# Second feed-forward block: the first sixteen inner tiles through the output weights as seven block products instead of eight, four tiles at a time

## The chip, the core and the metric

The kernel runs on one core of a Trainium2 chip. The metric is device time in microseconds (us); lower is better. The engines of the core are named as in the profile: PE (TensorE, matrix products; PEld is its weight load), DVE (VectorE), ACT (ScalarE), POOL (GpSimd), and SP, whose queue issues the loads. Each engine works through its own list of instructions.

## What is computed

One decoder block on 512 tokens of width 1024: a SwiGLU feed-forward, a token-mixing part and a second SwiGLU feed-forward, each with a modulated RMSNorm in front and a gated residual behind. The change concerns the second feed-forward alone:

```python
def swiglu(u, w_in, w_out):
    a, b = jnp.split(u @ w_in, 2, axis=-1)
    return (jax.nn.silu(a) * b) @ w_out
...
u = modulate(rmsnorm(h, g_norm_ffn2[l]), sh3, sc3)
h = h + 0.5 * gt3 * swiglu(u, w_ffn2_in[l], w_ffn2_out[l])
```

Here `w_in` is 1024 x 5632 and `w_out` 2816 x 1024. All data is float32.

## The kernel before

**Layout.** Features lie on the 128 partitions and the 512 tokens along the free dimension. The residual is eight tiles `H[m]` of 128x512, the normed input eight tiles `UH[k]`/`UL[k]`, and the 2816 inner features make 22 inner tiles.

**Split products.** Each float32 operand is a sum of two parts that TensorE reads as `fp32r`: a high part, made by ACT as a copy (`whi<-raw` for weights, `HI<-hf` for inner tiles), and a low part, made by DVE as the operand minus its high part (`wlo<-raw,whi`, `HK<-hf,HI`). A product is three matmuls: high x high, high x low, low x high.

**Weight stream.** Weights come in chunks of mostly 128x1024. SP loads a chunk into one of a few `raw` buffers (three, and two more, printed as `X`, from the first block product on). `split` then makes its two parts in a ring that holds seven chunks: `split_hi` issues the ACT copy and, if the next chunk is itself a difference of loaded chunks, DVE's subtraction for it (`make`, printed `X<-raw,X`); `split_lo` issues the DVE part. `look(4)`, called ahead of each product, runs this to four chunks ahead of the product about to be issued. `look()` runs three ahead.

**Inner tiles by seven products.** Inner tiles 0 to 3 are computed plainly (`ffn_pair`). From tile 4 on, `duo(j)` makes tiles j and j+1 at once: the inputs and weights are cut into 2x2 blocks, and seven block products replace eight. Each product is 24 matmuls on 256 tokens and uses one chunk, of which four are differences. The banks A, B and C of PSUM collect the products in the order A, B, A, C, A, B, A. Between two products on A its sum so far has to be copied out by ACT: after product 0 (`bank<-bank`, A into C), after product 2 (`u<-bank`) and after product 4 (`u<-bank` again). After product 1 the sum on B is copied (`p<-bank`). The next product on that bank, two products on for A, waits for the copy.

**Deferred work.** `later(n, f)` puts f aside until n more calls of `step()`, which comes after each product. The multiplication of a duo's two tiles (`hf<-sl,hf`) comes one step later, the high part and the low part two steps later.

**Output pass.** The inner tiles go through `w_out` in `PARTS` of 4, 4, 4, 4 and 6 tiles. Before the change each of the first four parts is a plain pass: eight output tiles, four inner tiles, three matmuls on 512 tokens, 96 matmuls and four chunks; DVE adds each result to `H[m]` with the gate (`H<-bank,mod,H`). In the program of before, the plain pass of part 0 follows the plain pairs directly; each later part is preceded by one duo of the next tiles (`pairs_before`). The last part ends the program and is not touched.

**Order.** `manual_schedule` keeps the instructions of each engine in the order in which the Python code issues them. Semaphore waits are put in from the tiles that are read and written.

Of the kernel before, what the change touches and what calls it, by code (L numbers as in the profile page):

```python
# [12 lines left out]
OP = mybir.AluOpType  # L13
# [33 lines left out]
def _fmajor(w, cols):  # L47
    k = w.shape[0] // P
    return w[:, cols].reshape(k, P, len(cols)).transpose(1, 0, 2).reshape(P, -1)
# [3 lines left out]
    return [np.arange(s, s + P) for s in starts]  # L53


def lay_ffn(w_in, w_out, first, plain):

    ins, outs = [], []  # L60
    if first:
        cols = np.concatenate([c for j in range(first) for c in _tiles(j * P, DFF + j * P)])
        for k in range(KT):
            ins.append(w_in[k * P:(k + 1) * P][:, cols])
    for j in range(first, plain):
        for c in _tiles(j * P, DFF + j * P):
            ins.append(_fmajor(w_in, c))
    for j in range(plain, FT, 2):
        for i, c in ((0, 0), (0, DFF), (1, DFF), (1, 0)):
            rows = w_in[i * D // 2:(i + 1) * D // 2]  # L70
            ins.append(np.concatenate([_fmajor(rows, x) for x in _tiles(c + j * P, c + j * P + P)], axis=1))
    for k0, k1 in PARTS:
        for m in range(KT):
            outs.append(_fmajor(w_out[k0 * P:k1 * P], np.arange(m * P, (m + 1) * P)))
    n = KT * (len(PARTS) - 1)
    return ins, [np.concatenate(outs[i:i + 2], axis=1) for i in range(0, n, 2)] + outs[n:]

# [59 lines left out]
class Kernel:  # L137
# [6 lines left out]
    def plan(self):  # L144
# [495 lines left out]

    def ffn_post(self, j, s, pb):
        nc = self.nc
        h = self.fw.tile([P, T], F32, name=("hf", "u3")[j % 2])
        nc.vector.tensor_tensor(h, s, pb, op=OP.mult)
        hh, hl = self.HH[j % NH], self.HL[j % NH]
        nc.scalar.activation(hh, h, AF.Copy)
        nc.vector.tensor_tensor(hl, h, hh, op=OP.subtract)

    def ffn_silu(self, j, pa):
        s = self.fw.tile([P, T], F32, name=("sl", "u2")[j % 2])  # L650
        self.nc.scalar.activation(s, pa, AF.Silu)
        return s

# [69 lines left out]
    def duo(self, j, first, last):  # L723
# [13 lines left out]
        c = self.fw.tile([P, 2 * T], F32, name="hf")  # L737
        u2, u3, p5 = (self.fw.tile([P, T], F32, name=x) for x in ("u2", "u3", "p5"))
        q = lambda x: x.rearrange("p (j h t) -> p j h t", j=2, h=2)
        r = lambda x: x.rearrange("p (j t) -> p j t", j=2)  # L740
        silu = lambda h, bank: nc.scalar.activation(q(s)[:, :, h, :], r(bank), AF.Silu)

        def mult():
            v.tensor_tensor(c, s, c, op=OP.mult)

        def high():
            copy(self.HHall[:, j % NH * T:(j % NH + 2) * T], c)

        def low():
            x = slice(j % NH * T, (j % NH + 2) * T)  # L750
            v.tensor_tensor(self.HLall[:, x], c, self.HHall[:, x], op=OP.subtract)


        for i, (bank, u, start) in enumerate(((A, blk(lo4, T1), True), (B, S[0], True), (A, S[1], False),
                                              (C, blk(hi4, T1), False), (A, S[2], False), (B, S[3], False),
                                              (A, blk(hi4, T2), False))):
            if i == 6:
                v.tensor_tensor(q(c)[:, :, 1, :], r(u3), r(p5), op=OP.add)
            self.look(4)
            self.product(bank, u, start)  # L760
            self.step()
            if i == 0:
                copy(C, A)
                if first:
                    first()
                    self.free += self.rawx
            elif i == 1:
                copy(p5, B)
            elif i == 2:
                copy(u2, A)  # L770
            elif i == 3:
                silu(0, C)
            elif i == 4:
                copy(u3, A)
            elif i == 6:
                silu(1, A)
                v.tensor_tensor(q(c)[:, :, 0, :], r(B), r(u2), op=OP.add)
        if last:
            mult()
            high()  # L780
# [1 line left out]
        else:  # L782
            self.later(1, mult)
            self.later(2, high)
            self.later(2, low)

    def ffn2(self):
        self.put, self.now = [], 0
        bk = [self.nb() for _ in range(4)]
        self.head(2, bk, AF.Silu)  # L790
        self.todo, last = self.u_steps(2)
# [33 lines left out]
    def ffn(self, n, j, last=None):  # L825
# [10 lines left out]
        for part, (k0, k1) in enumerate(PARTS):  # L836
            tail = part + 1 == len(PARTS)
            while j < pairs_before(n, part):
                if j < PLAIN[n]:
                    self.ffn_pair(j, beside)  # L840
                    j += 1
                else:
                    self.duo(j, last, tail and j + 2 == FT)
                    last = None
                    j += 2
            if n == 0:
                last = self.beside_out(part) or last
            nk = k1 - k0
            hk = [(self.HH[k % NH], self.HL[k % NH]) for k in range(k0, k1)]
            if not tail:  # L850
                for m in range(0, KT, 2):
                    self.look(4)
# [492 lines left out]
    def build(self):  # L1345
# [39 lines left out]
        with self.open_ffn():  # L1385
            self.ada_pool = ExitStack()
            self.adaw = self.ada_pool.enter_context(tc.tile_pool(name="f1a", bufs=4))
            self.put, self.now = [], 0
            self.startup()
            self.ffn(0, FIRST)  # L1390
            self.sums.close()
# [132 lines left out]
def lay_inputs(x, c, positions, w_ada, b_ada, g_norm_ffn1, w_ffn1_in, w_ffn1_out, g_norm_mix, w_in, w_pool,  # L1524
# [4 lines left out]
    f1i, f1o = lay_ffn(A(w_ffn1_in)[0], A(w_ffn1_out)[0], FIRST, PLAIN[0])  # L1529
    f2i, f2o = lay_ffn(A(w_ffn2_in)[0], A(w_ffn2_out)[0], 0, PLAIN[2])  # L1530
    wp = np.zeros((P, 2 * P), np.float32)
    for g in range(4):
        r = 64 * (g % 2)
# [30 lines left out]
```

## Time and profile before

| | us |
|---|---|
| median of 3 runs (lowest, highest) | 1017.11 (1016.72, 1018.24) |
| span of the profiled execution | 1018.4 |
| second feed-forward: first input matmul to last output matmul | 667.2 to 1007.9 |
| plain inner tiles 2 and 3 | 691.4 to 713.2 |
| plain output pass of part 0 | 713.2 to 734.9 |
| three duos (tiles 4 to 9) | 734.9 to 792.7 |
| output passes of parts 1, 2, 3 start at | 792.7, 853.0, 913.3 |
| last part starts at | 973.6 |

The profiled execution lies 1.3 us above the median of the runs; both are of the same program. A view by windows gives each engine's busy time in a stretch. The timeline gives start and duration of single instructions; the duration of one runs some 0.08 us into the next one of the same DVE or ACT, so two that follow each other directly start a little less than one duration apart. For matmuls the distance of two starts is the time that counts, since they are pipelined.

### The profile page before, as it was taken

Reading aid. Unit: us, or ns where it says so; the run is one execution under the profiler, and the core shown is the slowest. Engines: PE = TensorE matmul, PEld = TensorE weight load, DVE = VectorE, ACT = ScalarE, POOL = GpSimd, SP = SyncE. Lnnn points to the kernel's source line nnn. Section 1 sums busy time; section 2 is a strip of 40 time slices with the busy share of each in tenths; the row PEclk is TensorE's granted clock in tenths of the full one; section 3 lists DMA queues with packets and bytes.
Section 4 is the critical chain, followed back from the end, with each engine's and each line's share of the span. In section 5 each row is a group of like instructions: output and inputs, shape, how many; then the busy total and the mean of one; then the engine's idle time right before and its main releaser. Section 6 shows DMA issues by size and latency. Waiting matters only on the chain.

```text
span 1018.4 us, 15580 instructions
## 1 busy us (share of the span) xinstructions
PE 1007.5 (99%) x6364; PEld 913.3 (90%) x6364; DVE 756.1 (74%) x1112; ACT 437.2 (43%) x668; POOL 26.2 (3%) x30
## 2 busy tenths in 40 slices
PE   8999999999999999999999999999999999999997
PEld 7888898989999999889988888998899899998997
DVE  6979879889786776879447776577787776676764
ACT  5453352625444552233414323364366254352553
POOL 0000000000000000007100000000000000000001
PEclk9999999999999999999999999999999999999998
DMA  8856465455533413122154773312243234241312
GB/s 314 287 196 246 136 211 176 175 168 174 168 111 112 147 46 104 52 83 83 32 198 167 248 271 121 117 53 78 88 168 123 80 105 145 84 144 44 111 34 83
DMA packets 43114, 139.61 MB, mean 137 GB/s; under 512 B 4897, under 2 KB 8225, under 8 KB 43042
## 3 DMA queue, kind: packets, MB, share of 16 engines
q1 hardware_dynamic: 42354, 137.95, 40.8%
q8 instruction: 50, 0.82, 0.3%
q10 hardware_dynamic: 688, 0.66, 0.2%
q14 instruction: 22, 0.18, 0.1%
HBM read 135.82 MB, written 2.77 MB: 136 GB/s over the span
## 4 chain that ended last, share of the span: by engine, by line
PE 94%; DVE 4%; ACT 0%; issue 0%; DMA 0%; DVEq 0%; ACTq 0%
PE bank L337 17%; PE bank L338 17%; PE bank L339 17%; PE bank L719 10%; PE bank L721 10%; PE bank L720 10%; PE bank L1494 1%; PE bank L1496 1%; PE bank L1498 1%; PE bank L1090 1%; PE bank L1269 1%; PE bank L1423 1%; PE bank L1270 1%; PE bank L1271 1%; PE bank L1038 1%; DVE wlo L306 1%
## 5 line engine op out<-in xcount | busy, mean ns | idle before, releaser
L306 DVE TENSOR_TENSOR wlo<-raw,whi 128x1024 fp32r<-128x1024 f32 (+6 forms) x173 | 177.4, 1037 | 67.6 <-ACT whi L294 67.1
L294 ACT ACTIVATE whi<-raw 128x1024 fp32r<-128x1024 f32 (+6 forms) x173 | 152.3, 899 | 40.6 <-DVE raw L240 39.0
L337 PE MATMUL bank<-UH,whi 128*128 128x512 f32 (+1 forms) x432 | 158.3, 366 | 0.0
L338 PE MATMUL bank<-UL,whi 128*128 128x512 f32 (+1 forms) x432 | 154.2, 357 | 0.1
L339 PE MATMUL bank<-UH,wlo 128*128 128x512 f32 (+1 forms) x432 | 154.1, 357 | 0.0
L337 PE MATMUL bank<-HI,whi 128*128 128x512 f32 (+1 forms) x406 | 146.6, 361 | 0.0
L338 PE MATMUL bank<-HK,whi 128*128 128x512 f32 (+1 forms) x406 | 146.3, 360 | 0.0
L339 PE MATMUL bank<-HI,wlo 128*128 128x512 f32 (+1 forms) x406 | 146.2, 360 | 0.0
L721 PE MATMUL bank<-UH,wlo 128*128 128x256 f32 x512 | 141.6, 277 | 0.0
L719 PE MATMUL bank<-UH,whi 128*128 128x256 f32 x512 | 141.6, 277 | 0.0
L720 PE MATMUL bank<-UL,whi 128*128 128x256 f32 x512 | 141.6, 277 | 0.0
L306 DVE TENSOR_TENSOR wlo<-X,whi 128x1024 fp32r<-128x1024 f32 (+4 forms) x96 | 105.3, 1103 | 39.0 <-ACT whi L294 38.7
L719 PE MATMUL bank<-SH,whi 128*128 128x256 f32 x384 | 107.1, 279 | 0.1
L720 PE MATMUL bank<-SL,whi 128*128 128x256 f32 x384 | 107.0, 279 | 0.0
L721 PE MATMUL bank<-SH,wlo 128*128 128x256 f32 x384 | 106.9, 278 | 0.0
L294 ACT ACTIVATE whi<-X 128x1024 fp32r<-128x1024 f32 (+4 forms) x96 | 89.9, 958 | 32.1 <-DVE X L240 28.9
L720 PEld LDWEIGHTS bank<-UL,whi 128*128 128x128 f32 x512 | 96.3, 188 | 0.3
L719 PEld LDWEIGHTS bank<-UH,whi 128*128 128x128 f32 x512 | 96.1, 188 | 0.3
L721 PEld LDWEIGHTS bank<-UH,wlo 128*128 128x128 f32 x512 | 96.1, 188 | 0.0
L339 PEld LDWEIGHTS bank<-UH,wlo 128*128 128x128 f32 x432 | 81.3, 188 | 12.1
L338 PEld LDWEIGHTS bank<-UL,whi 128*128 128x128 f32 x432 | 81.2, 188 | 11.7 <-issue 0.5
L337 PEld LDWEIGHTS bank<-UH,whi 128*128 128x128 f32 x432 | 81.2, 188 | 11.3 <-issue 0.5
(225 smaller groups left out, 1746.4 us busy)
## 6 DMA issues: line engine op xcount, KB each, us to landing
ada<-wada SPq DMA_DIRECT2D x47, 512.0 KB, 5.0
raw<-wmix SPq DMA_DIRECT2D x44, 512.0 KB, 3.6
raw<-wf1i SPq DMA_DIRECT2D x34, 512.0 KB, 4.3
raw<-wf2i SPq DMA_DIRECT2D x30, 512.0 KB, 3.5
X<-wf2i SPq DMA_DIRECT2D x14, 512.0 KB, 3.6
cs<-wada SPq DMA_DIRECT2D x12, 512.0 KB, 3.5
AR<-wada SPq DMA_DIRECT2D x12, 512.0 KB, 4.0
raw<-wf2o SPq DMA_DIRECT2D x12, 512.0 KB, 3.6
```

Of the source, the lines that this page charges most:

```text
L294: self.nc.scalar.activation(self.hi[:, y], r[:, x], AF.Copy)
L306: self.nc.vector.tensor_tensor(self.lo[:, y], r[:, x], self.hi[:, y], op=OP.subtract)
L337: M(ps, hi, uh, start=start, stop=False)
L338: M(ps, hi, ul, start=False, stop=False)
L339: M(ps, lo, uh, start=False, stop=stop)
L719: M(o, hi, uh, start=start and p == 0 and k == 0, stop=False, skip_group_check=True)
L720: M(o, hi, ul, start=False, stop=False, skip_group_check=True)
L721: M(o, lo, uh, start=False, stop=k == 3, skip_group_check=True)
L1038: M(S[:, o + i * P:o + i * P + P], qz[:, (2 * i + h) * P:(2 * i + h + 1) * P], k[:, toks], start=True, stop=True)
L1090: M(o, pt[:, blk * P:blk * P + P], v, start=i == 0, stop=i == len(srcs) - 1)
L1269: M(b, self.UH[k][:, c::4], hi, start=k == 0, stop=False)
L1270: M(b, self.UH[k][:, c::4], lo, start=False, stop=False)
```

## The change

The first four output passes of the second feed-forward become `out_quad(k0, gate)`. The four inner tiles and the 512 x 1024 block of output weights are cut into 2x2 blocks, and seven products of 24 matmuls on 256 tokens replace the 96 matmuls on 512 tokens. A sum now fills two banks, so each copy of a bank becomes two. The four sums of inner blocks that the products need are made by `h_sums(k0)`: each is a DVE addition, an ACT high part and a DVE low part. They are put aside with `later` and so fall between the products of the duo that comes ahead of the pass. For part 0 there is now such a duo too. A duo whose second half of tokens is only needed as a sum leaves out the high and low part of that half. Products of inner tiles are kept in `self.kept`, which reuses three tiles that are free by then (`cond`, `cs`, `AR`). Of each four output weight chunks four differences are made, as for the duos, and the whole stream of part 0 to 3 is chunks for seven products.

```diff
     def plan(self):
...
-                plain(outs[part * KT // 2:(part + 1) * KT // 2] if part + 1 < len(PARTS) else outs[-KT:])
+                put = blocks if n and part + 1 < len(PARTS) else plain
+                put(outs[part * KT // 2:(part + 1) * KT // 2] if part + 1 < len(PARTS) else outs[-KT:])
...
 def pairs_before(n, part):
...
-    return k1 if part + 1 == len(PARTS) or (n == 2 and part == 0) else k1 + 2
+    return k1 if part + 1 == len(PARTS) else k1 + 2
...
     def duo(self, j, first, last):
...
+        ts = slice(0, 1 if self.kept and j % 4 == 0 and j < PARTS[-1][0] else 2)
...
+    def h_sums(self, k0):
...
+        def add(o, x, y, op):
+            v.tensor_tensor(o, x, y, op=op)
+
+        def high(i, s):
+            nc.scalar.activation(to[i][0], s, AF.Copy)
+
+        def low(i, s):
+            v.tensor_tensor(to[i][1], s, to[i][0], op=OP.subtract)
+
+        for n, what in enumerate(((lambda: add(h22, h21, h22, OP.add), lambda: high(0, h22)),
+                                  (lambda: add(h21, h11, h21, OP.subtract), lambda: high(2, h21), lambda: low(0, h22)),
+                                  (lambda: add(h11, h22, h11, OP.subtract), lambda: high(1, h11), lambda: low(2, h21)),
+                                  (lambda: add(h12, h12, h11, OP.subtract), lambda: high(3, h12), lambda: low(1, h11)),
+                                  (lambda: low(3, h12),))):
+            for f in what:
+                self.later(2 + n, f)
+
+    def out_quad(self, k0, gate):
...
+        def product(banks, u, start):
+            w = self.take()
+            for m in range(4):
+                o = banks[m // 2][:, m % 2 * HT:m % 2 * HT + HT]
+                for k in range(2):
+                    (hi, lo), (uh, ul) = w[2 * m + k], u[k]
+                    M(o, hi, uh, start=start and m % 2 == 0 and k == 0, stop=False, skip_group_check=True)
+                    M(o, hi, ul, start=False, stop=False, skip_group_check=True)
+                    M(o, lo, uh, start=False, stop=k == 1, skip_group_check=True)
+
+        def to_h(m, src, t):
+            h = self.H[m][:, t]
+            v.scalar_tensor_tensor(h, src, gate[:, m:m + 1], h, op0=OP.mult, op1=OP.add)
+
+        for i, (bank, u, start) in enumerate(((A, blk(k0, T1), True), (B, G[0], True), (A, G[1], False),
+                                              (C, blk(k0 + 2, T1), False), (A, G[2], False), (B, blk(k0, T2), False),
+                                              (A, blk(k0 + 2, T2), False))):
+            if i == 6:
+                for b in range(2):
+                    v.tensor_tensor(D[b][:, :, 1, :], p5[b], D[b][:, :, 1, :], op=OP.add)
+            self.look(4)
+            product(bank, u, start)
+            self.step()
+            for b in range(2):
+                if i == 0:
+                    copy(C[b], A[b])
+                elif i == 1:
+                    copy(p5[b], r(B[b]))
+                elif i == 2:
+                    copy(D[b][:, :, 0, :], r(A[b]))
+                elif i == 3:
+                    for m in (2 * b, 2 * b + 1):
+                        to_h(m, C[b][:, m % 2 * HT:m % 2 * HT + HT], T1)
+                elif i == 4:
+                    copy(D[b][:, :, 1, :], r(A[b]))
+                elif i == 5:
+                    v.tensor_tensor(D[b][:, :, 0, :], r(B[b]), D[b][:, :, 0, :], op=OP.add)
+        for m in range(4):
+            to_h(m, A[m // 2][:, m % 2 * HT:m % 2 * HT + HT], T2)
+        for m in range(4):
+            d = D[m // 2][:, m % 2, :, :].rearrange("p h t -> p (h t)")
+            self.later(1 + m // 2, lambda m=m, d=d: to_h(4 + m, d, slice(0, T)))
...
     def ffn(self, n, j, last=None):
...
                 else:
+                    if self.kept and not tail and j == k1:
+                        self.h_sums(k0)
                     self.duo(j, last, tail and j + 2 == FT)
...
+            if not tail and n:
+                self.out_quad(k0, gate)
+                continue
```

Left out are the layout of the weights on the host, the reuse of tiles for `kept`, and places in `duo` where views of tiles change without another instruction.

**ACT in the duo of tiles 16 and 17**, from the high part of the duo before it to about product 4. `u` and `p` are copies of banks, `sl` is the SiLU, `whi` the next weight chunks. Before:

```order
L726 ACTIVATE HI<-hf 128x1024
L726 ACTIVATE p_7630<-bank_100 128x512
L294 ACTIVATE whi<-X 128x896
L294 ACTIVATE whi<-X 128x128
L726 ACTIVATE u_7628<-bank_99 128x512
L294 ACTIVATE whi<-X 128x1024
L741 ACTIVATE sl<-bank_101 128x2x256
L294 ACTIVATE whi<-raw_68 128x1024
L726 ACTIVATE u_7629<-bank_99 128x512
```

and after (`ut`, and the last `HI`, are the high parts of the four sums of `h_sums`):

```order
L735 ACTIVATE HI<-cs 128x1024
L820 ACTIVATE ut<-cs 128x512
L735 ACTIVATE p_7961<-bank_97 128x512
L303 ACTIVATE whi<-X 128x1024
L820 ACTIVATE ut<-cond 128x512
L735 ACTIVATE u_7962<-bank_99 128x2x256
L303 ACTIVATE whi<-X 128x1024
L820 ACTIVATE ut<-cond 128x512
L758 ACTIVATE sl<-bank_102 128x2x256
L303 ACTIVATE whi<-X 128x1024
L820 ACTIVATE HI<-cs 128x2x256
L735 ACTIVATE u_7962<-bank_99 128x2x256
```

Ahead of each copy of a bank now stands the high part of a sum.

**DVE in the same duo**, from the multiplication of the duo before it. Before:

```order
L744 TENSOR_TENSOR hf<-sl,hf 128x1024
L240 TENSOR_TENSOR X<-X 128x1024
L306 TENSOR_TENSOR wlo<-raw_67,whi 128x1024
L751 TENSOR_TENSOR HK<-hf,HI 128x1024
L306 TENSOR_TENSOR wlo<-X,whi 128x896
L306 TENSOR_TENSOR wlo<-X,whi 128x128
L306 TENSOR_TENSOR wlo<-X,whi 128x1024
L306 TENSOR_TENSOR wlo<-raw_68,whi 128x1024
```

and after (the rows of L817 are the additions of `h_sums`, those of L823 its low parts):

```order
L761 TENSOR_TENSOR cs<-sl,cs 128x1024
L249 TENSOR_TENSOR X<-raw_66,X 128x1024
L315 TENSOR_TENSOR wlo<-raw_68,whi 128x1024
L769 TENSOR_TENSOR HK<-cs,HI 128x1024
L817 TENSOR_TENSOR cs<-cond,cs 128x2x256
L315 TENSOR_TENSOR wlo<-X,whi 128x1024
L817 TENSOR_TENSOR cond<-cond 128x2x256
L823 TENSOR_TENSOR G_5879<-cs,ut 128x512
L249 TENSOR_TENSOR X<-X 128x1024
L315 TENSOR_TENSOR wlo<-X,whi 128x1024
L817 TENSOR_TENSOR cond<-cs,cond 128x2x256
L823 TENSOR_TENSOR G_5883<-cond,ut 128x512
```

Each addition stands behind the low part of a weight chunk, and that one behind the addition of the step before.

**ACT from plain tile 3 into the duo of tiles 4 and 5**, after the change (before, the plain output pass lies between the second `HI` and the copy of a bank):

```order
L655 ACTIVATE HI<-cs 128x512
L303 ACTIVATE whi<-X 128x1024
L660 ACTIVATE p_5992<-bank_97 128x512
L303 ACTIVATE whi<-X 128x1024
L655 ACTIVATE HI<-cs 128x512
L303 ACTIVATE whi<-raw_68 128x1024
L303 ACTIVATE whi<-raw_66 128x896
L303 ACTIVATE whi<-raw_66 128x128
L735 ACTIVATE bank_101<-bank_99 128x512
```

The copy of product 0 of the duo (last row) now stands behind three weight chunks and the high part of tile 3.

More of the change, by code (lines that the diff above doesn't have):

```diff
@@ L53, in _tiles, with lay_ffn @@
     return [np.arange(s, s + P) for s in starts]
-def lay_ffn(w_in, w_out, first, plain):
+def lay_ffn(w_in, w_out, first, plain, blocks):
     ins, outs = [], []
@@ L71, in lay_ffn @@
             ins.append(np.concatenate([_fmajor(rows, x) for x in _tiles(c + j * P, c + j * P + P)], axis=1))
+    quads = []
     for k0, k1 in PARTS:
+        if blocks and k1 < FT:
+            for i, c in ((0, 0), (0, 4), (1, 4), (1, 0)):
+                rows = w_out[(k0 + 2 * i) * P:(k0 + 2 * i + 2) * P]
+                quads.append(np.concatenate([_fmajor(rows, x) for x in _tiles(*((c + m) * P for m in range(4)))], axis=1))
+            continue
         for m in range(KT):
             outs.append(_fmajor(w_out[k0 * P:k1 * P], np.arange(m * P, (m + 1) * P)))
+    if blocks:
+        return ins, quads + outs
     n = KT * (len(PARTS) - 1)
@@ L649, in ffn_silu @@
     def ffn_silu(self, j, pa):
-        s = self.fw.tile([P, T], F32, name=("sl", "u2")[j % 2])
+        s = self.fw.tile([P, T], F32, name="sl" if j % 2 == 0 else "u2" if not self.kept else "p5")
         self.nc.scalar.activation(s, pa, AF.Silu)
@@ L767, in duo @@
             elif i == 1:
-                copy(p5, B)
+                copy(p5, r(B))
             elif i == 2:
-                copy(u2, A)
+                copy(u2, r(A))
             elif i == 3:
@@ L787, in ffn2 @@
     def ffn2(self):
         self.put, self.now = [], 0
+        self.kept = [self.cond, self.cs, self.AR]
         bk = [self.nb() for _ in range(4)]
         self.head(2, bk, AF.Silu)
+        self.G = [(self.tp.tile([P, T], F32R, name="ut"), self.fw.tile([P, T], F32R, name=f"G{i}")) for i in range(3)]
         self.todo, last = self.u_steps(2)
```

50 lines of the change are left out of this document (39 added, 11 removed).

## The prediction

> **What bounds the kernel now.** The page's busy times and the chain that ended last come first, then who PE waited for.
>
> ```profile
> span 1018.4 us, 15580 instructions
> PE 1007.5 (99%) x6364; PEld 913.3 (90%) x6364; DVE 756.1 (74%) x1112; ACT 437.2 (43%) x668; POOL 26.2 (3%) x30
> ...
> PE 94%; DVE 4%; ACT 0%; issue 0%; DMA 0%; DVEq 0%; ACTq 0%
> ```
>
> ```profile
> PE bank L1416 <- ACT cond L1414: 3.3, 1, 3.3
> PE bank L1067 <- ACT prob L1055: 0.3, 1, 0.3
> ```
>
> PE is the bound everywhere: 94% of the chain, and its only long wait is 3.3 us at the start. So in the changed stretch fewer matmuls are a gain in full and each wait of PE a loss in full. Next the windows over one period of a plain output pass and two duos.
>
> ```profile
> 853.00:874.80 21.80, 21.80 (x99) 18.04 (x98) 15.17 (x16) 6.63 (x7) 0.00 (x0) 1.00 0.18 53
> 874.80:894.00 19.20, 19.20 (x169) 19.20 (x168) 13.92 (x14) 8.77 (x12) 0.00 (x0) 1.00 0.31 111
> 894.00:913.30 19.30, 19.30 (x172) 19.30 (x170) 14.23 (x16) 11.26 (x15) 0.00 (x0) 1.00 0.47 150
> ```
>
> PE is full at a granted clock of 1.00. DVE (third pair) has 43.3 of the 60.3 us, ACT 26.7.
>
> **What PE saves.** The starts of matmuls (first and last of the stretches) give their prices.
>
> ```profile
> 852.98 0.40 PE L337 MATMUL bank<-HI,whi 128*128 128x512 f32 x1
> ...
> 874.77 0.28 PE L719 MATMUL bank<-UH,whi 128*128 128x256 f32 x1
> ...
> 877.59 0.28 PE L719 MATMUL bank<-SH,whi 128*128 128x256 f32 x1
> ...
> 896.82 0.28 PE L719 MATMUL bank<-SH,whi 128*128 128x256 f32 x1
> ...
> 899.68 0.29 PE L719 MATMUL bank<-SH,whi 128*128 128x256 f32 x1
> ...
> 902.41 0.28 PE L719 MATMUL bank<-UH,whi 128*128 128x256 f32 x1
> ...
> 913.29 0.40 PE L337 MATMUL bank<-HI,whi 128*128 128x512 f32 x1
> ```
>
> A plain pass is 21.79 us for 96 matmuls, 227 ns each. Products 3 to 6 of the duo take 10.88 us for 96 on 256 tokens, 113 ns each; product 1, the dearest, 2.86 us for 24, 119 ns each. The 168 matmuls of a quad cost 19.0 us at the one and 20.0 at the other. I take 19.05: the quad's chunks go through `blocks`, which places them in the ring as for the duos, and six of a duo's seven products run at or near 113. Saved: 4 x 2.74 = 11.0 us, and 0.3 more, since a duo's first product lasts 2.82 us behind a plain pass (874.77 to 877.59) and 2.72 behind products. At the dear price it would be 7.2.
>
> **What DVE and ACT get.** Prices: 1024 elements start 1.14 us apart on DVE (rows below), and these groups give the smaller ones.
>
> ```profile
> L758 DVE TENSOR_TENSOR hf<-u,p 128x512 f32<-128x512 f32 x9 | 6.2, 686 | 0.0
> L863 DVE SCALAR_TENSOR_TENSOR H<-bank,mod,H 128x512 f32<-128x512 f32 x25 | 18.5, 749 | 20.0 <-PE bank L339 20.0
> L489 DVE SCALAR_TENSOR_TENSOR H<-bank,mod,H 128x256 f32<-128x256 f32 x10 | 4.8, 482 | 4.5 <-PE bank L339 4.5
> ```
>
> Less the 0.08 us by which neighbours overlap that is 0.60, 0.67 and 0.40. Per quad DVE gets three more low parts and four `make` (7 x 1.14 = 8.0), eight instructions for the sums less half a low part (4.3), four additions of sums of products (2.4), and eight updates of H of 256 and four of 512 instead of eight of 512 (0.5): 15.2 us. 43.3 + 15.2 = 58.5 us per period, against 57.4 of PE (two duos of 19.2 and a quad). So DVE is full, and for four periods that alone would leave 4 x (60.3 - 58.5) = 7.2 of the 11.3 us. ACT rises by three weight chunks (2.9), four high parts (2.0) and eight copies (4.0) to some 36 us: no bound as a sum. SP's list holds the same loads, with part 0's output chunks behind those of tiles 4 and 5; the windows' DMA share of 0.18 to 0.47 leaves room, but for the one load below.
>
> **Where PE would wait.** Sums don't settle it, since both engines go through their lists in order. I walk the second duo of a period, whose product 0 ends at 896.82 us. These are its ACT and DVE rows.
>
> ```profile
> 898.47 1.04 ACT L726 ACTIVATE HI<-hf 128x1024 fp32r<-128x1024 f32 x1
> 899.94 0.60 ACT L726 ACTIVATE p<-bank 128x512 f32<-128x512 f32 x1 [0.43 <-PE bank L721]
> 900.43 1.14 ACT L294 ACTIVATE whi<-X 128x896 fp32r<-128x896 f32 x2
> 902.67 0.60 ACT L726 ACTIVATE u<-bank 128x512 f32<-128x512 f32 x1 [1.10 <-PE bank L721]
> 903.17 1.05 ACT L294 ACTIVATE whi<-X 128x1024 fp32r<-128x1024 f32 x1
> 908.05 0.60 ACT L726 ACTIVATE u<-bank 128x512 f32<-128x512 f32 x1 [1.11 <-PE bank L721]
> ```
>
> ```profile
> 897.02 1.22 DVE L744 TENSOR_TENSOR hf<-sl,hf 128x1024 f32<-128x1024 f32 x1
> 898.15 1.22 DVE L240 TENSOR_TENSOR X<-X 128x1024 f32<-128x1024 f32 x1
> 899.29 1.22 DVE L306 TENSOR_TENSOR wlo<-raw,whi 128x1024 fp32r<-128x1024 f32 x1
> 900.42 1.22 DVE L751 TENSOR_TENSOR HK<-hf,HI 128x1024 fp32r<-128x1024 f32 x1
> 901.56 1.09 DVE L306 TENSOR_TENSOR wlo<-X,whi 128x896 fp32r<-128x896 f32 x1
> ```
>
> Now ACT's `u` starts 0.26 us after product 2 has ended, and product 4, at 902.41 + 2.72 = 905.13, finds it done. In the changed lists the first sum stands on DVE where the row of 901.56 stands, and ends 0.69 later, at 902.25. Its high part stands on ACT ahead of the `p` copy, so that copy, 899.94 now, starts only at 902.8. Behind it come the next chunk's high part, on DVE its low part, and behind that the second sum, whose high part holds up the `u` copy. This is a loop, run through three times: sum 0.69, high part 0.54, copy 0.49, chunk high part 1.05, chunk low part 1.14, three hand-overs of 0.03: 4.0 us, where PE's product takes 2.72. The 0.54 and the hand-over are from these rows.
>
> ```profile
> 710.22 0.68 DVE L644 TENSOR_TENSOR hf<-sl,bank 128x512 f32<-128x512 f32 x1
> ...
> 711.60 0.69 DVE L647 TENSOR_TENSOR HK<-hf,HI 128x512 fp32r<-128x512 f32 x1 [0.70 <-ACT HI L646]
> ```
>
> ```profile
> 710.93 0.63 ACT L646 ACTIVATE HI<-hf 128x512 fp32r<-128x512 f32 x1 [2.73 <-DVE hf L644]
> 711.47 1.05 ACT L294 ACTIVATE whi<-raw 128x1024 fp32r<-128x1024 f32 x1
> ```
>
> The sums end at 902.25, 906.2, 910.2 and 914.2. The `u` copy of product 2 ends 1.17 behind the second (0.03 + 0.54 + 0.60), at 907.4; 2.3 us late for product 4. That of product 4 ends at 915.35; product 6 would start two products behind 905.13, at 910.57. With 0.1 for PE to start again, 4.9 us lost in this duo. The `make` of steps 3 and 4 fit beside ACT's part of the loop (2.1 us against 0.6 + 1.14). Through the quad and the next duo the walk finds no wait: each copy is done 1.4 us or more ahead of its product, and DVE, 2 to 5 us behind in the quad, has caught up at the next period's start. If the four sums were covered, the loss would be nil; if the lateness carried on into the quad, a copy could cost one product more.
>
> The first quad is worse. Its duo now follows plain tile 3 at once, where the output pass of part 0 had let DVE catch up.
>
> ```profile
> 709.08 1.22 DVE L306 TENSOR_TENSOR wlo<-raw,whi 128x1024 fp32r<-128x1024 f32 x1
> ...
> 715.12 0.68 DVE L644 TENSOR_TENSOR u<-u,bank 128x512 f32<-128x512 f32 x1
> ```
>
> ```profile
> 713.18 0.39 PE L337 MATMUL bank<-HI,whi 128*128 128x512 f32 x1
> ```
>
> ```profile
> raw<-wf2i SPq DMA_DIRECT2D x30, 512.0 KB, 3.5
> ```
>
> 713.18 becomes the duo's start. Two `make` (2.3 us) come in ahead on DVE and use up 0.6 us of its waits, so tile 3's multiplication goes from 715.12 to 716.8 and its high part to 717.5. The low part of a chunk two instructions ahead of that multiplication ends at 715.7 and frees the buffer that the duo's fourth chunk needs, so that is loaded 3.5 later, at 719.2. Two chunks' high parts (1.05, 1.14) follow until 721.2, and only then the copy of product 0, done at 721.8, while product 2 would start at 713.18 + 2.82 + 2.86 = 718.9: 3.0 late. Behind it ACT has the split of an input block that `duo` does once here (1.05, to 722.8); then DVE has its low part, a `make` and a chunk's low part (3 x 1.14) and the first sum (0.69), which ends at 726.9; one loop and 1.17 later the `u` copy ends, at 732.0, against 727.3 for product 4: 4.8 more; two loops later product 6 waits 2.5 more. Together 10.3 us, between 4.9 (as the others) and 13.
>
> [...]
>
> **Sum.** -11.3 + 3 x 4.9 + 10.3 = +13.7 us on the profiled 1018.4, or 1032.1. That execution lies 1.3 above the median of 1017.1, so 1030.8 there: 1031.
>
> **Rivals.**
> - *Covered.* PE runs four chunks ahead, so a late DVE is only a sum of work: 4 x 1.8 = 7.2 to 11.3 us faster, 1006 to 1010. For it: PE waited nowhere in this stretch, with ACT under half busy. Against it: the lists, where a copy that PE needs stands behind a sum. It decides if the first sum ends 4.9 us earlier.
> - *Half.* DVE gets through the first sum one product (2.7 us) earlier than I walk: 3 x 2.2 and 4.9 lost, 11.3 saved: 1017, no change, or with the long first duo 1022.
> - *Carried on.* The lateness goes into the quads and one more product is lost in each: 4 x 2.7 = 10.8, 1042. For it: DVE's 58.5 us against 57.4. Against it: PE's own waits give DVE 4.9 us per period to catch up.
>
> **Chances.** As walked 0.68 (own range 1025 to 1037: the first duo between 4.9 and 13, the quads at the dear price 3.8 more), covered 0.09, half 0.13, carried on 0.10. The range takes in the walk, the half case's upper part and the carried-on case's lower part: 1018 to 1040. What this kernel's measurement can tell from no change is about 0.2%. Faster: 0.09 and a little of half, 0.11; same 0.05; slower 0.84.
>
> **What would show it.** In the duos of tiles 4, 8, 12 and 16: waits of PE on the ACT line of the bank copies, at products 4 and 6, 2.3 to 2.5 us each, and ACT waiting for L817 of DVE ahead of those copies. Quads of 19.05 us with no wait; duos of 6, 10, 14, 18 as before. If PE waits for `wlo` instead, or in the quads, the lateness is one of DVE's work as a whole. If it waits nowhere, the loop is not one, and I am wrong by 25 us.

## The result and the profile after

The changed kernel takes 1033.97 us (median of four runs, 1032.81 to 1037.16), the one before 1017.67 us in the runs beside it (1016.72 to 1019.89): a ratio of 1.0162, with a 95% interval of 1.014 to 1.0184. It is slower by 16.3 us; 1031 was forecast, within 1018 to 1040.

The page of the changed kernel, with its span, the busy times and the chain that ended last:

```profile
span 1031.0 us, 16299 instructions
...
PE 1003.5 (97%) x6652; PEld 922.5 (89%) x6652; DVE 815.2 (79%) x1206; ACT 474.5 (46%) x730; POOL 26.2 (3%) x30
...
PE 81%; DVE 10%; ACT 4%; issue 3%; DMA 0%; SPq 0%; DVEq 0%; ACTq 0%
```

PE is busy 4 us less in all (1003.5 for 1007.5) and yet the span grew. The chain says where to look: 13 points of it went from PE to DVE, ACT and issue. The view of waits names those that PE waited for (in all, how often, the longest, in us):

```profile
PE bank L728 <- ACT u L735: 13.5, 8, 2.9
PE bank L1527 <- ACT cond L1525: 3.3, 1, 3.3
PE bank L728 <- ACT bank L735: 2.9, 1, 2.9
```

The wait of 3.3 us at the start was there before. The others are new: nine waits on ACT's copies of banks in `duo`. The next view is of windows, one for each duo of tiles 4, 8, 12 and 16 with the quad behind it, and the duos between them (length, then busy time of PE, PEld, DVE, ACT and POOL, the granted clock, the DMA share, GB/s):

```profile
710.16:739.87 29.71, 23.39 (x169) 22.78 (x168) 24.23 (x28) 16.52 (x23) 0.00 (x0) 0.89 0.35 118
739.87:758.91 19.04, 19.04 (x170) 19.04 (x169) 19.00 (x24) 12.54 (x18) 0.00 (x0) 1.00 0.33 111
758.91:778.11 19.20, 19.20 (x170) 19.20 (x169) 19.17 (x24) 10.02 (x13) 0.00 (x0) 1.00 0.34 111
778.11:802.31 24.20, 21.48 (x170) 21.08 (x169) 19.72 (x24) 13.34 (x19) 0.00 (x0) 0.93 0.26 87
802.31:821.35 19.04, 19.04 (x170) 19.04 (x169) 19.01 (x24) 12.55 (x18) 0.00 (x0) 1.00 0.35 111
821.35:840.55 19.20, 19.20 (x170) 19.20 (x169) 19.17 (x24) 10.03 (x13) 0.00 (x0) 1.00 0.33 111
840.55:866.12 25.57, 21.13 (x170) 20.74 (x169) 21.08 (x25) 13.34 (x19) 0.00 (x0) 0.94 0.26 83
866.12:885.42 19.30, 19.30 (x170) 19.30 (x169) 18.42 (x24) 12.40 (x18) 0.00 (x0) 0.99 0.34 110
885.42:904.62 19.20, 19.20 (x171) 19.20 (x169) 19.17 (x23) 10.10 (x13) 0.00 (x0) 1.00 0.33 111
904.62:928.78 24.16, 21.27 (x171) 20.88 (x169) 19.22 (x23) 13.35 (x19) 0.00 (x0) 0.93 0.27 88
928.78:947.82 19.04, 19.04 (x171) 19.04 (x169) 19.01 (x23) 12.85 (x18) 0.00 (x0) 1.00 0.34 112
```

The quads are what was forecast: 19.04 us three times and 19.30 once, PE full. The loss is in the four duos ahead of them. Those between take 19.2 us as before. A duo without waits takes 19.2 (19.3 behind plain tile 3), so 10.4, 5.0, 6.4 and 5.0 us are lost; with 0.25 in the third quad, 27.0 us. Less 11.3 saved that is 15.7.

The two spans differ by 12.6 only, and the reason is a way of reading that serves for all runs below. Up to the change PE does the same in both kernels, but it got there at 713.18 us in the profiled execution of before and at 710.16 here. Over the profiled executions of all kernels in the table below this point lies between 709.29 and 713.18 us, and the runs of one kernel spread as much (those of before from 1016.72 to 1019.89 us). From there to the end before took 1018.4 - 713.18 = 305.2 us and this kernel 320.8: 15.6 more, as the windows say.

ACT's rows in the duo that starts at 904.62 (start, length, engine, line, operation; in brackets the idle time before, and whom it waited for):

```profile
912.89 0.63 ACT L820 ACTIVATE ut<-cs 128x512 fp32r<-128x512 f32 x1 [2.86 <-DVE cs L817]
913.42 0.58 ACT L735 ACTIVATE p<-bank 128x512 f32<-128x512 f32 x1
913.90 1.05 ACT L303 ACTIVATE whi<-X 128x1024 fp32r<-128x1024 f32 x1
916.85 0.63 ACT L820 ACTIVATE ut<-cond 128x512 fp32r<-128x512 f32 x1 [1.89 <-DVE cond L817]
917.39 0.58 ACT L735 ACTIVATE u<-bank 128x512 f32<-128x512 f32 x1
...
924.77 0.63 ACT L820 ACTIVATE HI<-cs 128x512 fp32r<-128x512 f32 x1 [1.90 <-DVE cs L817]
925.31 0.58 ACT L735 ACTIVATE u<-bank 128x512 f32<-128x512 f32 x1
```

and DVE's in the same duo:

```profile
912.16 0.69 DVE L817 TENSOR_TENSOR cs<-cond,cs 128x512 f32<-128x512 f32 x1
914.99 1.23 DVE L315 TENSOR_TENSOR wlo<-X,whi 128x1024 fp32r<-128x1024 f32 x1 [2.13 <-ACT whi L303]
916.13 0.68 DVE L817 TENSOR_TENSOR cond<-cond 128x512 f32<-128x512 f32 x1
...
920.09 0.68 DVE L817 TENSOR_TENSOR cond<-cs,cond 128x512 f32<-128x512 f32 x1
...
924.05 0.69 DVE L817 TENSOR_TENSOR cs<-cs,cond 128x512 f32<-128x512 f32 x1
```

Read them in turns. ACT stands 2.86 us before the high part of a sum, with the copy of a bank behind it and the next chunk's high part behind that (912.89 to 914.95); DVE meanwhile stands 2.13 us before that chunk's low part (914.99), and only then comes to the next sum (916.13), for which ACT waits again. The engines wait for one another, and a turn takes 3.96 us (sums at 912.16, 916.13, 920.09, 924.05).

### The profile page after: what moved, and what is told of

It reads as the page before. It is cut to its first block, busy times and chain, and to the rows that moved or that the text cites. A ratio compares the mean times of both kernels' runs of the same rounds, so it can differ in the third digit from the quotient of the medians.

```text
span 1031.0 us, 16299 instructions
## 1 busy us (share of the span) xinstructions
PE 1003.5 (97%) x6652; PEld 922.5 (89%) x6652; DVE 815.2 (79%) x1206; ACT 474.5 (46%) x730; POOL 26.2 (3%) x30
## 4 chain that ended last, share of the span: by engine, by line
PE 81%; DVE 10%; ACT 4%; issue 3%; DMA 0%; SPq 0%; DVEq 0%; ACTq 0%
PE bank L346 14%; PE bank L347 14%; PE bank L348 13%; PE bank L728 7%; PE bank L730 7%; PE bank L729 7%; PE bank L855 2%; PE bank L856 2%; PE bank L854 2%; DVE wlo L315 2%; PE bank L1605 1%; PE bank L1609 1%; PE bank L1607 1%; ACT whi L303 1%; PE bank L1201 1%
## 5 line engine op out<-in xcount | busy, mean ns | idle before, releaser
L315 DVE TENSOR_TENSOR wlo<-raw,whi 128x1024 fp32r<-128x1024 f32 (+7 forms) x174 | 175.9, 1024 | 54.9 <-ACT whi L303 54.6
L303 ACT ACTIVATE whi<-raw 128x1024 fp32r<-128x1024 f32 (+7 forms) x174 | 151.7, 890 | 31.8 <-DVE raw L249 28.3
L315 DVE TENSOR_TENSOR wlo<-X,whi 128x1024 fp32r<-128x1024 f32 (+4 forms) x109 | 121.3, 1119 | 31.8 <-ACT whi L303 31.6
L303 ACT ACTIVATE whi<-X 128x1024 fp32r<-128x1024 f32 (+4 forms) x109 | 104.2, 973 | 46.6 <-DVE X L249 45.6
L728 PE MATMUL bank<-SH,whi 128*128 128x256 f32 x384 | 110.6, 288 | 12.5 <-ACT u L735 9.5
L729 PE MATMUL bank<-SL,whi 128*128 128x256 f32 x384 | 109.8, 286 | 0.0
L730 PE MATMUL bank<-SH,wlo 128*128 128x256 f32 x384 | 109.7, 286 | 0.0
L346 PE MATMUL bank<-HI,whi 128*128 128x512 f32 (+1 forms) x278 | 96.8, 348 | 0.0
L347 PE MATMUL bank<-HK,whi 128*128 128x512 f32 (+1 forms) x278 | 96.5, 347 | 0.0
L348 PE MATMUL bank<-HI,wlo 128*128 128x512 f32 (+1 forms) x278 | 96.4, 347 | 0.0
L348 PEld LDWEIGHTS bank<-UH,wlo 128*128 128x128 f32 x432 | 81.1, 188 | 12.1
```

The source lines that it names most:

```text
L303: self.nc.scalar.activation(self.hi[:, y], r[:, x], AF.Copy)
L315: self.nc.vector.tensor_tensor(self.lo[:, y], r[:, x], self.hi[:, y], op=OP.subtract)
L346: M(ps, hi, uh, start=start, stop=False)
L347: M(ps, hi, ul, start=False, stop=False)
L348: M(ps, lo, uh, start=False, stop=stop)
L728: M(o, hi, uh, start=start and p == 0 and k == 0, stop=False, skip_group_check=True)
```

## The experiments

In the table, "the stretch" runs from the start of the work behind plain tile 3 to the end of the span, as above. In the runs beside them the kernel before took 1017.16 us with the first four experiments, 1017.51 with the next two and 1017.35 with the last.

| kernel | median, us | ratio to before (95%) | starts at | span | stretch less 305.2 |
|---|---|---|---|---|---|
| the change | 1033.97 | 1.0162 (1.014 to 1.0184) | 710.16 | 1031.0 | +15.6 |
| high parts one step later | 1013.55 | 0.9964 (0.9948 to 0.9979) | 710.10 | 1010.9 | -4.4 |
| bank copies ahead of the steps | 1022.51 | 1.0049 (1.0034 to 1.0063) | 709.69 | 1020.6 | +5.7 |
| part 0 plain | 1026.87 | 1.0096 (1.0074 to 1.0118) | 709.64 | 1025.3 | +10.5 |
| no sums | 1010.30 | 0.9929 (0.9914 to 0.9945) | 710.07 | 1008.7 | -6.6 |
| high parts later, part 0 plain | 1007.93 | 0.9903 (0.9888 to 0.9919) | 709.29 | 1005.9 | -8.6 |
| high parts later, first copy early | 1014.90 | 0.9965 (0.9950 to 0.9979) | 712.96 | 1013.2 | -5.0 |
| the same, first quad's sums later | 1012.89 | 0.9961 (0.9946 to 0.9976) | 709.67 | 1010.1 | -4.8 |

**High parts one step later.** The theory: it is the loop, not the amount of work, that costs. Each high part moves one step behind its addition (and the low part one more), so that DVE has a product's time for the sum before ACT asks for it. No instruction is added or left out.

```diff
-        for n, what in enumerate(((lambda: add(h22, h21, h22, OP.add), lambda: high(0, h22)),
-                                  (lambda: add(h21, h11, h21, OP.subtract), lambda: high(2, h21), lambda: low(0, h22)),
...
+        for n, what in enumerate(((lambda: add(h22, h21, h22, OP.add),),
+                                  (lambda: add(h21, h11, h21, OP.subtract), lambda: high(0, h22)),
+                                  (lambda: add(h11, h22, h11, OP.subtract), lambda: high(2, h21), lambda: low(0, h22)),
...
+                                  (lambda: high(3, h12), lambda: low(1, h11)),
```

> Edit: in h_sums each high part is issued one step behind its addition, and each low part one step behind that; nothing is added or left out. Theory (the loop of sum, high part, bank copy, chunk high part and chunk low part sets PE's waits): the bank copies no longer stand behind a sum that DVE has yet to make, so the duos of tiles 8, 12 and 16 lose nothing (19.2 us instead of 24.2 to 25.6); the duo of tile 4 keeps its 3.0 us wait for the copy of product 0 and about 1 to 2 us more. 11.3 us saved, some 4.5 lost: about 1011. Rival A (DVE's sum of work, 58.5 us per period against 57.4): 1 us or more lost per period wherever the instructions stand, and PE waits for wlo: 1014 or more. Rival B (the sums only tip over a lateness that is there anyway): 1025 or more.

PE's waits in the second block of this kernel:

```profile
PE bank L728 <- ACT bank L735: 2.9, 1, 2.9
PE bank L728 <- ACT u L735: 0.9, 2, 0.5
```

The eight waits of 13.5 us have become two with 0.9 in all, and those lie in the duos of tiles 6 and 18, behind quads. The duos of tiles 8, 12 and 16 take 19.2 us. The stretch is 20.0 us shorter with the same work on every engine: the loss was the order of the rows. What stays is the wait for the copy of product 0 in the first duo, 2.9 us.

**Bank copies ahead of the steps.** A second way out of the loop: in this block's duos the step's work (sums, high parts) stands behind the copy of the bank instead of ahead of it.

```diff
-            self.step()
+            if not self.kept:
+                self.step()
             if i == 0:
                 copy(C, A)
...
+            if self.kept:
+                self.step()
```

> Edit: in the second feed-forward's duos step() is called behind the bank copy of the product instead of ahead of it, so the copy stands on ACT ahead of the high part of a sum; the loop itself keeps its length. Theory: the copy of a product now waits for the sum of one step earlier only; walked with the same prices about 0.4 us lost at product 4 and 1.4 at product 6, so 1.9 per duo instead of 4.9, and some 6 in the duo of tile 4: about 1018. If the length of the loop alone counted and not the copy's place in it: 1030 or more. If the copy's place were all: 1011, as with the later high parts.

PE's waits in the second block:

```profile
PE bank L728 <- ACT u L735: 8.1, 10, 1.5
PE bank L728 <- ACT bank L735: 2.9, 1, 2.9
```

By the starts of matmuls, waits of 0.5 us at product 4 (1.6 in the first duo) and 1.2 to 1.4 at product 6 are left in the four duos: the copy still stands behind the high part of the step before, so the loop is shortened and not cut. The time is 4.5 us over what I had worked out. By the starts of matmuls about 2 us of that are in the quads (19.2 to 19.8 us for 19.04, with waits of 0.3 at most; the matmuls start 114 to 118 ns apart instead of 113), and 1.9 in the duos between (19.3 to 20.0 us for 19.2), two of which have a wait of 0.5 to 0.6 us. Why the quads' matmuls start further apart here was not settled.

**Part 0 plain.** Parts 1 to 3 go through quads, part 0 through the plain pass, with no sums in its duo.

```diff
-                put = blocks if n and part + 1 < len(PARTS) else plain
+                put = blocks if n and 0 < part < len(PARTS) - 1 else plain
...
-            if not tail and n:
+            if not tail and n and part:
                 self.out_quad(k0, gate)
```

> Edit: part 0 goes back to the plain output pass with its chunks, ahead of the duo of tiles 4 and 5; parts 1 to 3 stay quads. Theory (the first quad's duo loses 10.4 us because it follows plain tile 3 without DVE having caught up, the others 5.0 to 6.4): 8.4 us saved on PE, some 16 lost: about 1025, and no wait of PE for the copy of product 0 in the duo of tile 4. Rival (each quad costs the same, a quarter of 16 us): 1030.

PE's only waits in the second block:

```profile
PE bank L728 <- ACT u L735: 13.0, 6, 2.2
```

The wait for the copy of product 0 is gone, the three loops stay with two waits each. The first duo's 10.4 us less the 3.0 that its quad had saved should give back 7.4; the stretch got 5.1 shorter. The difference is in the other duos (1.5) and in a quad of 19.8 us (0.7).

**No sums.** `h_sums` is left out: the quads take the tiles' own high and low parts as operands, so the four additions, high and low parts are not done, and what this kernel computes is no longer the block.

```diff
...
-                    if self.kept and not tail and j == k1:
-                        self.h_sums(k0)
```

> Edit: h_sums is left out; the three products of a quad that need sums read inner tiles in their place, and every duo makes the high and low parts of both halves of tokens, so the second feed-forward's output is not the reference's. All matmuls, chunks, differences of chunks and bank copies stay. Theory: the duos of tiles 8, 12 and 16 last 19.2 us, the duo of tile 4 keeps the 3.0 us wait at product 0 with some clock loss behind it: about 1009 to 1010. Rival (the differences of chunks and the quads' own additions are enough to make DVE late): 1015 or more.

All quads take 19.04 us, all duos behind the first 19.2. The only wait of the second block is again the 2.9 us (3.07 between the matmuls) for the copy of product 0 in the duo of tiles 4 and 5. So the saving on PE is real: 11.3 less 4.7 in that duo (24.04 us for 19.3) is 6.6, and the stretch is 6.6 shorter. And the sums themselves, once out of the loop, cost 2.2 us (this kernel against the first experiment).

**High parts later, part 0 plain.** The first and third edits together.

> As the run with the high parts one step later, but the output pass of part 0 (tiles 0 to 3) stays plain, so three quads instead of four. My theory: there PE's only wait of 2.9 us for a copy is that of product 0 of tiles 4 and 5, and it comes from having no plain pass between tile 3 and this duo. With the plain pass kept, that wait and the stretch at half speed behind it (3.0 and 1.5 us) go, and one quad's saving (2.7 us) is given back: 1013.6 - 4.5 + 2.7 = 1011.8, or, counted from the time before with three savings of 2.74 and 0.2, 1017.2 - 8.4 = 1008.8. I expect 1009 to 1012 us and no wait of PE over 1 us in the second block. Rival: the plain pass doesn't let DVE catch up any more, since the sums and low parts load it; then the 3 us wait comes back at product 0 of another duo, and the time is 1014 us or more.

Windows of this kernel: the plain pass of part 0, the duo behind it, and the first quad.

```profile
709.30:731.10 21.80, 21.80 (x98) 18.04 (x97) 17.17 (x20) 7.70 (x9) 0.00 (x0) 1.00 0.31 99
731.10:750.40 19.30, 19.30 (x169) 19.30 (x168) 14.96 (x15) 9.85 (x13) 0.00 (x0) 1.00 0.48 164
788.80:807.84 19.04, 19.04 (x170) 19.04 (x169) 19.00 (x24) 12.54 (x18) 0.00 (x0) 1.00 0.34 111
```

PE waits nowhere in the second block. The stretch is 8.6 us shorter than before, where three quads save 3 x 2.74 + 0.2 = 8.4. This is the fastest kernel here: 0.97% below the one before, 2.5% below the change, and a little faster than I had expected.

**First copy early.** To keep all four quads, the first duo's own wait has to go. In that duo the chunks that are prepared with product 0 come behind it and the copy of its bank (on top of the later high parts).

```diff
+            early = i == 0 and first and self.kept
+            if not early:
+                self.look(4)
             self.product(bank, u, start)
             self.step()
             if i == 0:
                 copy(C, A)
+                if early:
+                    self.look(4)
```

> As the run with the high parts one step later, and one more edit: in the duo of tiles 4 and 5 the weight chunks that are prepared ahead with product 0 come after product 0 and the copy of its bank, so that this copy stands ahead of three weight chunks on ACT. My theory: the 3.0 us wait of PE at product 2 of that duo is ACT's order alone; with the copy ahead of them it goes, and with it the stretch at half speed (1.5 us): 1013.6 - 4.5 = 1009.1, and down to 1007 if all four savings of 2.74 us and 0.3 are kept. I expect 1007 to 1010 us. Rival: the three chunks are late themselves (DVE's low part frees their buffer), so that PE waits for a low part instead, 2 to 3 us, and the time stays at 1012 us or more.

The longest wait of the second block, PE's row from the timeline:

```profile
727.52 0.58 PE L728 MATMUL bank<-SH,whi 128*128 128x256 f32 x1 [3.14 <-ACT u L735]
```

The wait at product 2 is gone and comes back at product 4, 3.1 us long. The window of this duo and DVE's row of the first sum say why.

```profile
712.96:738.54 25.58, 22.44 (x170) 22.21 (x168) 23.73 (x28) 16.80 (x23) 0.00 (x0) 0.87 0.42 139
```

```profile
725.63 0.68 DVE L821 TENSOR_TENSOR cs<-cond,cs 128x512 f32<-128x512 f32 x1
```

DVE is busy 23.73 of 25.58 us, and its first sum starts 12.7 us behind the duo's start; the `u` copy stands behind that sum's high part. My theory, that ACT's order alone made the wait, fell: the order decides where it stands, and DVE's lateness makes it.

**First quad's sums later.** On top of that, all of the first quad's sums one step later.

```diff
-                self.later(2 + n, f)
+                self.later(2 + n + (k0 == 0), f)
```

> As the run with product 0's copy ahead of the chunks, in which PE still waited 3.1 us, now at product 4 of the duo of tiles 4 and 5, for the copy that stands behind the first sum's high part; here all of h_sums stands one step later in the first quad alone (in the other three as in that run). My theory: DVE is behind in this duo whatever ACT's order, and each copy that stands ahead of the first high part is safe; with the sums one step later the copy of product 2 stands ahead of it, so no wait over 1 us is left, and 3.1 + 1.4 us (the stretch at half speed) go: 1014.9 - 4.5 = 1010.4, I expect 1008 to 1011.5 us. Rival: DVE's lateness comes up again one product later (the copy of product 4 behind the second high part), PE waits 2 to 3 us at product 6, and the time stays at 1013 us or more.

PE's waits on the bank copies:

```profile
PE bank L728 <- ACT u L735: 3.8, 4, 2.2
```

The wait moved again, by the starts of matmuls to 0.8 us at product 4 and 2.3 at product 6, and the first quad takes 20.1 us. The rival's place is the right one; the time lies just below its 1013. Over the three orders the wait between matmuls is 3.0 us (at product 2), 3.3 (at 4) and 3.2 (at 4 and 6 together): DVE is some 3 us behind there, and none of the three orders removes that. Of what was tried only the plain pass does, in which DVE has 4.6 us to spare (17.17 of 21.80 above). In the stretch these three kernels lie within 0.6 us of each other (-4.4, -5.0 and -4.8), so which of the orders is best is not shown.

**Graded waits.** Waits of PE were followed by matmuls at half the pace, for which the forecast's sum has no term. In the kernel before, product 2's bank is copied several times over in every duo, so that PE waits at product 4 for graded times; a second run has the lengths in another order.

```diff
             elif i == 2:
+                self.duos = getattr(self, "duos", -1) + 1
+                for _ in range((7, 11, 8, 12, 9, 13, 10, 14, 6)[self.duos % 9]):
+                    copy(u2, A)
                 copy(u2, A)
```

> The kernel before, with ACT's copy of product 2's bank done 7 to 15 times over in every duo of both blocks, so that PE waits at product 4 for graded times of some 1 to 6 us. A measurement of what follows a wait of PE, by its length: the starts of the next matmuls, 113 ns apart or some 200. Theory from the waits of the runs so far: none below 2 us is followed by a slow stretch, of those from 2.3 to 3.1 us some two in three, and all beyond 3.4; the stretch is about 3.3 us long and costs 1.5 us. [...]

> The same measurement with the lengths in another order, so that the same length falls at other times: if the length alone decides, each length behaves as in the other run; if it depends on when the wait falls, the same length goes both ways between 2 and 3.4 us.

Windows of the first run behind waits of 1.97, 2.60 and 3.22 us (the first row, the second, the third):

```profile
821.87:824.80 2.93, 2.93 (x25) 2.93 (x25) 2.12 (x3) 2.42 (x4) 0.00 (x0) 1.00 0.01 3
844.21:847.30 3.09, 3.09 (x14) 3.09 (x15) 1.94 (x3) 2.41 (x4) 0.00 (x0) 0.50 0.00 0
916.41:922.40 5.99, 5.99 (x28) 5.99 (x29) 2.45 (x2) 2.80 (x4) 0.00 (x0) 0.50 0.43 103
```

Behind the wait of 1.97 us the granted clock stayed at 1.00; behind those of 2.60 and 3.22 us it was 0.50, for 3.1 and 6.0 us. The longest wait of the run, 7.59 us, has 0.50 behind it too:

```profile
263.24 0.58 PE L719 MATMUL bank<-SH,whi 128*128 128x256 f32 x1 [7.59 <-ACT u L726]
```

```profile
263.24:266.20 2.96, 2.96 (x14) 2.96 (x15) 2.37 (x3) 2.41 (x4) 0.00 (x0) 0.50 0.04 7
```

Two windows of the second run have 0.50; which of its lengths went which way is not shown.

```profile
145.10:148.20 3.10, 3.10 (x14) 3.10 (x15) 2.19 (x3) 2.41 (x4) 0.00 (x0) 0.50 0.00 0
268.90:272.20 3.30, 3.26 (x15) 3.26 (x16) 2.67 (x4) 2.46 (x4) 0.00 (x0) 0.50 0.18 24
```

The lengths between 2.0 and 2.6 us stay open here; whether equal lengths go both ways there is read from the changed kernel, below.

## Why the prediction was right, and where its parts were not

- **The loop** (three duos, 4.9 us each) was right in place, mechanism and size. The sums were to end 8.15, 12.1, 16.1 and 20.1 us behind the duo's start; they end at 912.85, 916.81, 920.77 and 924.74, that is 8.2, 12.2, 16.2 and 20.1 behind 904.62. A turn was worked out as 4.0 and takes 3.96. The losses are 5.0, 6.4 and 5.0. For PE to start again behind a copy the walk had 0.1; by the rows it is 0.05 (the copy of 917.39 is done at 917.97, the matmul starts at 918.02). That it is the loop, and not DVE's work as a whole, is shown by the first experiment.
- **The saving** of 11.3 us was right: quads of 19.04 for 19.05, and without sums the stretch is shorter by just this, less the first duo's loss.
- **The first duo** was right in sum (10.4 for 10.3) and in its ends: the copy for product 4 was to be done 18.8 us behind its start and is at 18.9. Its split was not: waits of 3.0, 4.8 and 2.5 were forecast, and 3.0, 3.0 and 0.8 are there by the starts of matmuls. The row below and the next show what came between. The first wait was the copy of product 0, as walked,

```profile
718.89 0.39 PE L728 MATMUL bank<-SH,whi 128*128 128x256 f32 x1 [2.87 <-ACT bank L735]
```

  and behind it PE ran at half pace (a granted clock of 0.50 from 719.86 to 723.28 us), so that it came to product 4 some 1.7 us later and waited less there. The walk's reason for the first wait was half right: it named DVE's lost slack and the copy's place on ACT, and the two experiments on this duo show that the place only says at which product the lateness is paid. One link of the walk was not there at all. It had the duo's fourth chunk loaded only by 719.2, 6.0 us behind the duo's start, because its buffer would come free only with a low part two instructions ahead of tile 3's multiplication. These rows of the changed kernel say otherwise (SP's loads, then DVE, then ACT):

```profile
708.60 0.33 SPq L233 DMA_DIRECT2D raw<-wf2i  x1
719.54 0.33 SPq L233 DMA_DIRECT2D raw<-wf2o  x1
```

```profile
715.95 1.22 DVE L249 TENSOR_TENSOR raw<-raw,raw 128x1024 f32<-128x1024 f32 x1
```

```profile
717.21 1.15 ACT L303 ACTIVATE whi<-raw 128x896 fp32r<-128x896 f32 x2 [0.95 <-DVE raw L249]
718.26 0.58 ACT L735 ACTIVATE bank<-bank 128x512 f32<-128x512 f32 x1
```

  The chunk's load was issued at 708.60, before the duo began at 710.16, and the next one only at 719.54, when the copy of product 0 was done (718.84). What ACT waited for was DVE's `make` of 715.95, which stands behind tile 3's multiplication and low part. The copy is done 8.7 us behind the duo's start, for 8.6 in the walk. Since the walk came there by way of a load that held nothing up, it is in part luck that this wait came out at 3.0.
- **The clock.** The forecast's sum has no term for PE's clock. The granted clock fell to 0.50 behind five of six waits of 2.3 to 3.0 us, as in these rows:

```profile
918.02 0.58 PE L728 MATMUL bank<-SH,whi 128*128 128x256 f32 x1 [2.20 <-ACT u L735]
918.40 0.41 PE L729 MATMUL bank<-SL,whi 128*128 128x256 f32 x1
...
921.33 0.28 PE L728 MATMUL bank<-SH,whi 128*128 128x256 f32 x1
```

```profile
918.00:922.40 4.40, 4.38 (x25) 4.38 (x26) 4.01 (x5) 2.51 (x4) 0.00 (x0) 0.63 0.28 83
854.00:859.40 5.40, 5.40 (x47) 5.40 (x48) 4.61 (x6) 2.96 (x4) 0.00 (x0) 1.00 0.36 100
```

  Matmuls start 0.21 us apart for some 3.3 us, 1.5 us lost. Behind product 4's wait this costs next to nothing, since the loop sets when product 6 can start (there the wait is 0.6 to 0.9 instead of 2.3). Only in the duo of tiles 12 and 13 the clock stayed at 1.00 behind the first wait (854.00, the second row) and fell behind that of product 6, with no copy left to wait for: 1.5 us there and 0.25 in the quad. With 0.25 us of smaller differences these make up the 2 us between 25.0 us of losses forecast (10.3 and 3 x 4.9) and 27.0 measured.
- **No other waits**: the duos of tiles 6, 10, 14 and 18 take 19.2 us, and no lateness is carried out of the quads, as forecast; DVE, expected at 58.5 us per period, has 57.4 to 58.7 (the duo between, the duo with sums and its quad, rows above).

## What to carry to other kernels

When a helper engine's list has a copy that the bounding engine needs, standing behind an instruction that waits for another engine, draw the cycle: if that engine's next item waits for something behind the copy, the turn of the loop, and not the sum of either engine's work, sets the pace (here 3.96 us for a product's 2.72, with ACT at 46% and DVE at 79% of the span). The remedy is one step of distance between producing a value on one engine and asking for it on the other: the same instructions, 20 us less. And a wait that only moved when the waiter's list was reordered was made by another engine here: look for where that one loses its slack.

## What had not been expected of the hardware

- PE's granted clock fell to 0.50 behind five of the six waits of 2.3 to 3.0 us in the changed kernel, and behind none of its three waits of 0.6 to 0.9 us. Equal waits (2.41 us, ending at 791.56 and at 854.00) went both ways. From the first of these waits to the last matmul of this trace the granted clock changes at 719.86, 723.28, 730.10, 733.52, 791.54, 794.96, 863.22, 866.64, 917.84 and 921.25 us, each a whole multiple of 3.41 us behind the first. The next rows are four stretches between points that lie on these multiples.

```profile
788.13:791.54 3.41, 1.18 (x11) 0.99 (x9) 3.01 (x4) 1.52 (x4) 0.00 (x0) 1.00 0.09 35
791.54:794.96 3.42, 3.40 (x16) 3.40 (x17) 3.03 (x5) 1.53 (x3) 0.00 (x0) 0.50 0.07 22
849.57:852.98 3.41, 2.18 (x20) 1.99 (x18) 2.01 (x3) 1.51 (x3) 0.00 (x0) 1.00 0.41 167
852.98:856.39 3.41, 2.39 (x20) 2.39 (x21) 3.02 (x4) 1.91 (x3) 0.00 (x0) 1.00 0.02 5
```

  The wait that ends at 791.56 lies in one of them (first row), and in the next the clock is at 0.50 (second row). The one that ends at 854.00 is cut in two, 1.4 and 1.0 us, and the clock stays (third and fourth row). These are the stretches ahead of the other four falls.

```profile
716.45:719.86 3.41, 0.97 (x8) 0.97 (x9) 3.07 (x5) 2.65 (x5) 0.00 (x0) 1.00 0.00 0
726.69:730.10 3.41, 0.99 (x8) 0.99 (x9) 3.02 (x5) 2.06 (x3) 0.00 (x0) 1.00 0.65 256
859.81:863.22 3.41, 1.30 (x11) 1.30 (x12) 1.88 (x4) 2.47 (x4) 0.00 (x0) 1.00 0.00 0
914.42:917.84 3.42, 1.40 (x13) 1.20 (x11) 2.85 (x4) 1.53 (x3) 0.00 (x0) 1.00 0.18 74
```

  In this trace, from 20 to 1020 us, the five such stretches with 0.97 to 1.40 us of PE busy were each followed by one at 0.50, and no other has less than 2.18 us. So some 2 us without work in one of them were enough here, and the two waits of 2.41 us differ in how they lie against these points.
- In the kernel with the bank copies first the wait of 2.9 us for the copy of product 0 (view of waits above) was followed by no slow stretch; this is the window behind it. How that wait lay against the changes of the clock in its run is not shown.

```profile
718.40:723.90 5.50, 5.47 (x48) 5.48 (x48) 4.74 (x6) 2.76 (x4) 0.00 (x0) 1.00 0.58 155
```

- The quads' matmuls start 113 ns apart in the changed kernel (19.04 us for 168), and about 117 ns apart in a quad of the kernel with the bank copies first (19.78 us, the row below) and in the first quad of the kernel with the first quad's sums later (20.10 us, of which 0.4 are a wait). What differs there stays open.

```profile
735.52:755.30 19.78, 19.78 (x170) 19.78 (x169) 19.71 (x24) 13.14 (x20) 0.00 (x0) 1.00 0.35 107
```
